# Hybrid block: the first two weight tiles multiply unscaled, transposed x; the normed h is made meanwhile

## The chip, the cores and the metric

One core of a Trainium2 chip runs the whole layer in one launch. The metric is the device time of one execution in microseconds (us), the median of several runs.

## The reference

One layer over 512 tokens of 1024 features in float32: RMS norm, a wide input projection, a state-space branch (SSD) and a windowed attention branch, their gated merge, then a mixture of 64 experts. What matters here is the head:

```python
h = rms_norm(x, norm1_g)          # x * rsqrt(mean(x*x) + 1e-6) per token, times norm1_g per feature
proj = h @ w_in
z, xbc, dt_raw, q, k, v, g_ssd, g_att = jnp.split(proj, IN_SPLITS, axis=-1)
# ssd_branch
xbc = conv(xbc, conv_w, 4 taps, per channel) + conv_b
xbc = silu(xbc)
dt = softplus(dt_raw + dt_bias)
```

The factor of a token, rsqrt(mean(x*x) + 1e-6), is the same for all its features, so it can be applied before or after the product with w_in.

## The kernel before, in words

The projections keep features on the partitions and the 512 tokens along the free axis. For float32 precision on TensorE, each operand is split in two float32r parts, hi (a rounded copy, made by ScalarE) and lo (the remainder, made by VectorE or GpSimd), and a product is hi\*hi + hi\*lo + lo\*hi: three matmuls for each of the eight blocks of 128 features, 24 for an output of 128 x 512.

A weight tile is 128 x 2048 (1 MB) and serves two such outputs, its two halves. `proj` (L185) loads one tile into a `w` buffer (two of them), splits each half (`split`, L178, into `g` buffers, four of them), runs the 24 matmuls (L196 to L198) into a PSUM buffer `mm` (two of them) and hands it to `use`. In `split` the remainder is GpSimd's for the first two splits and then for each fifth one, else VectorE's.

The head of the kernel (L144 to L174): x comes by rows, four row tiles of two 512-column halves. Squares are summed on ScalarE (L160) and VectorE (L157), the factor is made on VectorE and GpSimd (L161, L124, L125), the rows are scaled (L163, L164), 32 transposes on TensorE (L169) turn them, and L171 and L172 leave the eight pairs `hh`, `hl` of h, times norm1_g.

`dt_stage` (L210 to L273) follows: 16 matmuls of h with the weights of dt (L219, L220), four small transposes, and then a chain of small operations, mostly VectorE's, that ends in dt, its cumulative sums and their exponentials. Then `xbc_stage(0)` takes weight tiles 0, 1 and 2: each of their six outputs goes through `conv` (L280), which reads PSUM once on ScalarE and three times on VectorE (L283), then a tanh on ScalarE and a product on VectorE (L287). Only after the third VectorE read is the `mm` buffer free. `ssd_main(0)` needs all six and dt (first at L346). `gate_stage`, the next groups, attention, the merge and the output projection follow, and then the experts, whose weights (192 MB) SyncE loads at L779 into buffers that come free as the earlier stages end.

Tiles come from pools with a fixed number of buffers for each tag (`x`, `h` and `y` have 16, `c` six). A planner at build time orders each engine's instructions by the order in the program and by when it expects them to be ready, so that neighbouring stages are interleaved; on the chip each engine keeps that order. DMAs that are issued from SyncE go through one queue, in order.

Of the kernel before, what the change touches and what calls it, by code (L numbers as in the profile page):

```python
# [7 lines left out]
F = mybir.dt.float32  # L8
# [5 lines left out]
OP = mybir.AluOpType  # L14
# [16 lines left out]
def tile_hybrid(ctx: ExitStack, tc: tile.TileContext, x, pos, cols, rows, g2d, wrd, wdtd, wcm, wqkv, wso, wao, wo,  # L31
# [112 lines left out]
    xs_ = []  # L144
    st = pb.tile([128, 16], F, name="st")
    for t in range(4):
        xt = [x_(), x_()]
        for u in range(2):
            nc.sync.dma_start(xt[u], x[t * 128:(t + 1) * 128, u * 512:(u + 1) * 512])
        xs_.append(xt)  # L150
    wdt = v_(n=256)
    nc.sync.dma_start(wdt, wdtd)
    for t in range(4):
        for u in range(2):
            jk = c_()
            if u:
                V.scalar_tensor_tensor(jk, xs_[t][u], 1.0, xs_[t][u], op0=OP.mult, op1=OP.mult,  # L157
                                       accum_out=st[:, 2 * t + u:2 * t + u + 1])
            else:
                S.activation(jk, xs_[t][u], AF.Square, accum_out=st[:, 2 * t + u:2 * t + u + 1])  # L160
        V.tensor_tensor(st[:, 8 + t:9 + t], st[:, 2 * t:2 * t + 1], st[:, 2 * t + 1:2 * t + 2], op=OP.add)  # L161
        rsq(st[:, 8 + t:9 + t], 1, 1.0 / 1024)
        V.tensor_scalar(xs_[t][0], xs_[t][0], st[:, 8 + t:9 + t], None, op0=OP.mult)  # L163
        S.activation(xs_[t][1], xs_[t][1], AF.Copy, scale=st[:, 8 + t:9 + t])  # L164
    hh, hl = [], []
    for k in range(8):
        p = ptile(("tp", "sb", "y", "tp")[k // 2])
        for t in range(4):
            T.transpose(p[:, t * 128:(t + 1) * 128], xs_[t][k // 4][:, (k % 4) * 128:(k % 4 + 1) * 128], ident)  # L169
        hi, lo = h_(), h_()  # L170
        S.activation(hi, p, AF.Copy, scale=n1g[:, k:k + 1])  # L171
        V.scalar_tensor_tensor(lo, p, n1g[:, k:k + 1], hi.bitcast(F), op0=OP.mult, op1=OP.subtract)  # L172
        hh.append(hi)
        hl.append(lo)  # L174
# [9 lines left out]

    def proj(src, mh, ml, use):  # L185
        raw = w_()
        parts = 1 if nsp[0] else 2
        for i in range(parts):
            c = slice(i * 2048 // parts, (i + 1) * 2048 // parts)
            nc.sync.dma_start(raw[:, c], src[:, c])  # L190
        for hf in range(2):
            hi, lo = split(raw[:, hf * 1024:(hf + 1) * 1024], 1024)
            p = ptile("mm")
            for k in range(8):
                s = slice(k * 128, (k + 1) * 128)
                T.matmul(p, hi[:, s], mh[k], start=(k == 0), stop=False)  # L196
                T.matmul(p, hi[:, s], ml[k], start=False, stop=False)  # L197
                T.matmul(p, lo[:, s], mh[k], start=False, stop=(k == 7))  # L198
            use(hf, p)

# [9 lines left out]
    def dt_stage():  # L210
        wd = g_()
# [63 lines left out]
    dt_stage()  # L275

# [12 lines left out]
    def xbc_stage(g, qs=range(3)):  # L289
        for i in qs:  # L290
            def use(hf, p, i=i):
                c = 6 * g + 2 * i + hf
                tl = b_() if i == 0 else x_()
                if i == 0:
                    bc[g, hf] = tl
                else:
                    xsT[4 * g + 2 * (i - 1) + hf] = tl
                conv(c, tl, p)
            proj(wcm[3 * g + i], hh, hl, use)
# [340 lines left out]
    xbc_stage(0)  # L640
# [577 lines left out]
def _layout(inp):  # L1218
# [14 lines left out]
    def tm(m):  # L1233
# [20 lines left out]
        ("x", c(f["x"][0])),  # L1254
        ("pos", c(f["positions"][0].reshape(4, 128).T)),
# [31 lines left out]
```

## Time and profile before

| | |
|---|---|
| median of 3 runs | 1229.57 us (1229.18 to 1230.66) |
| the profiled execution | 1228.64 us, of which the span of the trace is 1226.8 us |
| TensorE busy | 1136.3 us (93%) |
| VectorE busy | 656.5 us (54%) |
| ScalarE busy | 388.6 us (32%) |
| GpSimd busy | 239.3 us (20%) |
| moved by DMA | 273.86 MB, 223 GB/s on average |

Times in the rows are in us from the start of the span. PE is TensorE's matmuls, PEld its weight loads, DVE VectorE, ACT ScalarE, POOL GpSimd, SPq SyncE's queue. A row of the timeline has start, duration, engine, line, operation, output and input; in brackets stands the engine's idle time just before and what ended it. Matmuls overlap, so their pitch is less than the duration shown. Engines' busy shares are averages over stages with different limits, so the stage at hand counts.

### The profile page before, as it was taken

The page shows a single profiled execution, that of the slowest core. Times are in us where ns is not written, and L with a number is a line of the kernel's source. Part 1 is how long each engine was busy: PE and PEld are TensorE (multiplying, and loading weights), DVE is VectorE, ACT ScalarE, POOL GpSimd, SP SyncE. Part 2 cuts the span into 40 slices and gives each one's busy share as a digit, 9 for nine tenths or more (in the row PEclk, how much of TensorE's full clock was granted, in tenths as well). Part 3 has the DMA queues.
Part 4 walks back from the last instruction along what each step waited for, and adds up shares of the span by engine and source line. Part 5 has one row for each costly group of instructions (what it writes and reads, how often), then busy time and mean ns, then how long its engine had stood idle before and what let it go on. Part 6 is the DMA issues. An engine that isn't in the chain of part 4 may idle for free.

```text
span 1226.8 us, 16583 instructions
## 1 busy us (share of the span) xinstructions
PE 1136.3 (93%) x6552; PEld 772.2 (63%) x6552; DVE 656.5 (54%) x1224; ACT 388.6 (32%) x796; POOL 239.3 (20%) x195
## 2 busy tenths in 40 slices
PE   6999999999999999999999959999897899999885
PEld 5777778877878988988778956443342434434321
DVE  5958584569536678877665464634422233331422
ACT  5456453464326455634432311110110011111000
POOL 3033431143024533330120241001001001000100
PEclk9999999999999999999999989999999899999999
DMA  4231213221221222222357257999999999999995
GB/s 157 98 118 38 100 61 129 94 79 54 83 104 35 70 104 87 87 69 69 137 168 300 110 235 305 419 420 420 420 419 421 420 415 398 387 420 419 421 419 221
DMA packets 43120, 273.86 MB, mean 223 GB/s; under 512 B 5024, under 2 KB 5664, under 8 KB 11808
## 3 DMA queue, kind: packets, MB, share of 16 engines
q1 hardware_dynamic: 39744, 263.34, 54.1%
q0 software_dynamic: 1712, 7.34, 1.6%
q10 hardware_dynamic: 1584, 2.10, 0.6%
q8 instruction: 52, 0.85, 0.3%
q14 instruction: 28, 0.23, 0.1%
HBM read 266.47 MB, written 6.29 MB: 222 GB/s over the span
## 4 chain that ended last, share of the span: by engine, by line
PE 77%; DVE 10%; DMA 8%; issue 2%; ACT 2%; POOL 1%; SPq 0%; DVEq 0%; ACTq 0%; POOLq 0%
PE mm L196 11%; PE mm L198 11%; PE mm L197 11%; PE mm L904 11%; PE y L925 5%; PE tp L884 5%; DMA rb<-in_wgu_dram 3%; PE tp L1003 3%; DVE acc L1005 2%; PE mm L481 2%; PE tp L1004 2%; PE mm L480 2%; DMA ra<-in_wdn_dram 2%; DMA rb<-in_wdn_dram 2%; PE mm L482 2%
## 5 line engine op out<-in xcount | busy, mean ns | idle before, releaser
L196 PE MATMUL mm<-h,g 128*128 128x512 f32 x448 | 180.7, 403 | 0.8 <-DVE c L309 0.5
L197 PE MATMUL mm<-h,g 128*128 128x512 f32 x448 | 179.8, 401 | 0.0
L198 PE MATMUL mm<-h,g 128*128 128x512 f32 x448 | 178.5, 399 | 0.8 <-POOL g L182 0.8
L904 PE MATMUL mm<-rb,st 128*32 128x512 f32 x712 | 145.6, 619 | 13.3 <-DMA rb<-in_wgu_dram 13.3
L181 ACT ACTIVATE g<-w 128x1024 fp32r<-128x1024 f32 x100 | 105.6, 1057 | 139.4 <-PE mm L197 99.0
L182 DVE TENSOR_TENSOR g<-w,g 128x1024 fp32r<-128x1024 f32 x78 | 98.7, 1265 | 72.9 <-ACT g L181 69.9
L1005 DVE TENSOR_TENSOR acc<-acc,tp 128x512 f32<-128x512 f32 x132 | 86.1, 684 | 37.2 <-PE tp L1004 37.0
L993 POOL TENSOR_SCALAR wk<-dr,vcol 128x512 fp32r<-128x512 int16 x17 | 26.6, 1565 | 383.8 <-PE tp L1004 347.9
L198 PEld LDWEIGHTS mm<-h,g 128*128 128x128 f32 x448 | 84.4, 188 | 22.2 <-POOL g L182 1.5
L196 PEld LDWEIGHTS mm<-h,g 128*128 128x128 f32 x448 | 84.5, 189 | 20.3 <-issue 1.2
L197 PEld LDWEIGHTS mm<-h,g 128*128 128x128 f32 x448 | 84.5, 189 | 19.8 <-issue 1.7
L182 POOL TENSOR_TENSOR g<-w,g 128x1024 fp32r<-128x1024 f32 x22 | 53.8, 2446 | 169.3 <-ACT g L181 138.5
L904 PEld LDWEIGHTS mm<-rb,st 128*32 128x32 f32 x712 | 30.9, 113 | 79.9 <-issue 55.8
L925 PE MATMUL y<-rb,n 128*32 128x512 f32 x384 | 72.0, 641 | 4.0 <-ACT n L916 3.3
L904 PE MATMUL mm<-ra,st 128*32 128x512 f32 x312 | 75.5, 597 | 0.0
L884 PEld LDWEIGHTS tp<-oh,hx 128*128 128x128 f32 x480 | 60.1, 191 | 23.6 <-issue 14.9
L931 DVE TENSOR_TENSOR yo<-y,yo 128x512 fp32r<-128x512 f32 x34 | 23.5, 691 | 92.3 <-ACT yo L930 92.3
L884 PE MATMUL tp<-oh,hx 128*128 128x256 f32 x480 | 66.7, 289 | 3.9 <-DVE m L956 3.6
L1003 PE MATMUL tp<-yo,wk 128*128 128x512 f32 x132 | 59.2, 465 | 11.1 <-DVE acc L1005 11.0
L1003 PEld LDWEIGHTS tp<-yo,wk 128*128 128x128 f32 x132 | 23.6, 187 | 69.6 <-DVE acc L1005 39.2
L909 ACT ACTIVATE n<-mm,gts 128x256 f32<-128x256 f32 x17 | 8.0, 473 | 180.6 <-PE mm L904 161.7
L910 DVE SCALAR_TENSOR_TENSOR n<-n,mm 128x256 f32<-128x256 f32 x17 | 7.1, 421 | 92.6 <-ACT n L909 92.6
(378 smaller groups left out, 2269.4 us busy)
## 6 DMA issues: line engine op xcount, KB each, us to landing
rb<-in_wgu_dram SPq DMA_DIRECT2D x89, 1024.0 KB, 15.1
rb<-in_wdn_dram SPq DMA_DIRECT2D x48, 1024.0 KB, 17.8
ra<-in_wgu_dram SPq DMA_DIRECT2D x39, 1024.0 KB, 12.5
w<-in_wcm_dram SPq DMA_DIRECT2D x27, 1024.0 KB, 4.9
ra<-in_wdn_dram SPq DMA_DIRECT2D x16, 1024.0 KB, 18.1
w<-in_wso_dram SPq DMA_DIRECT2D x8, 1024.0 KB, 4.9
w<-in_wqkv_dram SPq DMA_DIRECT2D x6, 1024.0 KB, 4.8
gtd<-c POOLq DMA_DIRECT2D x16, 256.0 KB, 2.5
```

The costliest lines, as they stand in the source:

```text
L181: S.activation(hi[:, :n], src, AF.Copy)
L182: (G if nsp[0] < 3 or nsp[0] % POOL_LO == 0 else V).tensor_tensor(lo[:, :n], src, hi[:, :n].bitcast(F), op=OP.subtract)
L196: T.matmul(p, hi[:, s], mh[k], start=(k == 0), stop=False)
L197: T.matmul(p, hi[:, s], ml[k], start=False, stop=False)
L198: T.matmul(p, lo[:, s], mh[k], start=False, stop=(k == 7))
L480: T.matmul(o, hh[k][:, ts], hi[:, s], start=(k == 0), stop=False)
L884: T.matmul(p[:, u * 256:(u + 1) * 256], hx[h][:, t, (k + u) * 128:(k + u + 1) * 128], oh[:, t], start=(h == 0 and t == 0), stop=(h == 1 an ...
L904: T.matmul(pg[e * 32:(e + 1) * 32], sts[u // 2][:, k, c:c + 32], wt[u, k // 4, e][:, (k % 4) * 512:(k % 4 + 1) * 512], start=(k == 0), sto ...
L925: T.matmul(py[n][e * 32:(e + 1) * 32], hT[:, f * 128 + e * 32:f * 128 + e * 32 + 32], wt[u, 2, e][:, ws], start=(f == 0), stop=(f == 1))
L993: G.tensor_scalar(wk, drow[0], vcol[:, b:b + 1], None, op0=OP.is_equal)
L1003: T.matmul(p, wk[:, t * 128:(t + 1) * 128], yhl[n][0], start=True, stop=False)
L1005: V.tensor_tensor(acc[t][:, ns], acc[t][:, ns], p, op=OP.add)
```

## The change

A copy of x, transposed outside (`xtd`: eight blocks of 128 features by 512 tokens), is a new input. The loads at the head are reordered: the first quarter of weight tile 0, two blocks of transposed x, the second quarter, the other six blocks, the second half of tile 0, then x by rows. The blocks times norm1_g, without the tokens' factors, are split into `fh`, `fl` (`y` buffers). Tile 0 is multiplied with these into two `y` buffers of PSUM, and so is tile 1, through `proj`. The sums of squares are taken from x by rows, all four factors in one go; a product of ones with the factors on a diagonal spreads them over the partitions (`rb_`). The outputs of tiles 0 and 1 are multiplied by `rb_` on their way out of PSUM (into a `c` buffer), and `conv` reads that. h is made from the transposed blocks, norm1_g and `rb_`, and split as before, with every second remainder on GpSimd. The 32 transposes are gone. `dt_stage` now stands behind tiles 0 and 1 and ahead of tile 2, and loads its own weights. From tile 2 on all is as before.

```diff
-    xs_ = []
     st = pb.tile([128, 16], F, name="st")
-    for t in range(4):
-        xt = [x_(), x_()]
-        for u in range(2):
-            nc.sync.dma_start(xt[u], x[t * 128:(t + 1) * 128, u * 512:(u + 1) * 512])
-        xs_.append(xt)
-    wdt = v_(n=256)
-    nc.sync.dma_start(wdt, wdtd)
+    xT, xs_, w0 = [x_() for k in range(8)], [[x_(), x_()] for t in range(4)], w_()
+    nc.sync.dma_start(w0[:, 0:512], wcm[0][:, 0:512])
+    nc.sync.dma_start(xT[0], xtd[0])
+    nc.sync.dma_start(xT[1], xtd[1])
+    nc.sync.dma_start(w0[:, 512:1024], wcm[0][:, 512:1024])
+    for k in range(2, 8):
+        nc.sync.dma_start(xT[k], xtd[k])
+    nc.sync.dma_start(w0[:, 1024:], wcm[0][:, 1024:])
     for t in range(4):
         for u in range(2):
...
+            nc.sync.dma_start(xs_[t][u], x[t * 128:(t + 1) * 128, u * 512:(u + 1) * 512])
+    wdt = v_(n=256)
...
+    fh, fl = [], []
+    for k in range(8):
+        if k in (0, 4):
+            if k == 0:
+                whi, wlo = g_(), g_()
+            c = slice(k * 128, (k + 4) * 128)
+            S.activation(whi[:, c], w0[:, c], AF.Copy)
+            G.tensor_tensor(wlo[:, c], w0[:, c], whi[:, c].bitcast(F), op=OP.subtract)
+        hi, lo = y_(), y_()
+        S.activation(hi, xT[k], AF.Copy, scale=n1g[:, k:k + 1])
+        V.scalar_tensor_tensor(lo, xT[k], n1g[:, k:k + 1], hi.bitcast(F), op0=OP.mult, op1=OP.subtract)
+        fh.append(hi)
+        fl.append(lo)
+    p0_ = [ptile("y"), ptile("y")]
+    triple(whi, wlo, fh, fl, p0_[0])
+    triple(*split(w0[:, 1024:], 1024), fh, fl, p0_[1])
+
+    for t in range(4):
+        for u in range(2):
+            jk, a = c_(), st[:, 2 * t + u:2 * t + u + 1]
+            if u:
+                V.scalar_tensor_tensor(jk, xs_[t][u], 1.0, xs_[t][u], op0=OP.mult, op1=OP.mult, accum_out=a)
+            else:
+                S.activation(jk, xs_[t][u], AF.Square, accum_out=a)
+    V.tensor_reduce(st[:, 8:12], st[:, 0:8].rearrange("p (t u) -> p t u", u=2), axis=AX.X, op=OP.add)
+    rsq(st[:, 8:12], 4, 1.0 / 1024)
+    dg, rb_ = v_(), v_()
+    for t in range(4):
+        V.tensor_scalar(dg[:, t * 128:(t + 1) * 128], ident, st[:, 8 + t:9 + t], None, op0=OP.mult)
+    p = ptile("sb")
+    T.matmul(p, ones, dg, start=True, stop=True)
+    S.activation(rb_, p, AF.Copy)
+    hh, hl = [], []
+    for k in range(8):
+        V.scalar_tensor_tensor(xT[k], xT[k], n1g[:, k:k + 1], rb_, op0=OP.mult, op1=OP.mult)
+        hi, lo = h_(), h_()
+        S.activation(hi, xT[k], AF.Copy)
+        (G if k % 2 else V).tensor_tensor(lo, xT[k], hi.bitcast(F), op=OP.subtract)
+        hh.append(hi)
+        hl.append(lo)
...
     def dt_stage():
+        nc.sync.dma_start(wdt, wdtd)
...
-    def xbc_stage(g, qs=range(3)):
+    def xbc_stage(g, qs=range(3), first=False):
         for i in qs:
             def use(hf, p, i=i):
                 c = 6 * g + 2 * i + hf
+                if first:
+                    u = c_()
+                    V.tensor_tensor(u, p, rb_, op=OP.mult)
+                    p = u
...
-            proj(wcm[3 * g + i], hh, hl, use)
+            if first and i == 0:
+                for hf in range(2):
+                    use(hf, p0_[hf])
+            elif first:
+                proj(wcm[3 * g + i], fh, fl, use)
+            else:
+                proj(wcm[3 * g + i], hh, hl, use)
...
-    xbc_stage(0)
+    xbc_stage(0, qs=(0, 1), first=True)
+    dt_stage()
+    xbc_stage(0, qs=(2,))
     ssd_main(0)
```

The 24 matmuls of an output moved into a helper, `triple`, with the same three lines as L196 to L198, and `proj` always loads its tile in one DMA (before, the first tile came in two).

## Rows read from the trace of the kernel before

**Rows 1.** Mean rates: busy us (x instructions) by engine, clock, DMA share, GB/s, in two stretches.
```profile
core 0: us, PE busy (x) PEld busy (x) DVE busy (x) ACT busy (x) POOL busy (x), PEclk, DMA share, GB/s
50.00:100.00 50.00, 50.00 (x239) 39.12 (x238) 33.44 (x64) 27.03 (x49) 11.43 (x10) 1.00 0.26 92
750.00:800.00 50.00, 48.51 (x307) 24.82 (x304) 25.25 (x56) 8.18 (x15) 6.35 (x5) 1.00 1.01 418
```

**Rows 2.** Waits of SyncE's queue, whole span: us in total, times, longest.
```profile
SPq L779 <- PE mm L738: 38.9, 2, 38.4
```

**Rows 3.** Waits of TensorE, first 60 us: us in total, times, longest.
```profile
PE tp L169 <- DVE x L163: 9.6, 3, 8.3
PE mm L198 <- POOL g L182: 0.8, 1, 0.8
```

**Rows 4.** Timeline of TensorE: start us, us, what, idle before and its releaser.
```profile
8.31 0.69 PE L169 MATMUL tp<-ident,x 128*128 128x128 f32 x2 [8.31 <-DVE x L163]
...
15.57 0.66 PE L219 MATMUL mm<-h,g 128*128 128x512 f32 x1
...
28.42 0.50 PE L198 MATMUL mm<-h,g 128*128 128x512 f32 x1 [0.76 <-POOL g L182]
28.76 0.40 PE L196 MATMUL mm<-h,g 128*128 128x512 f32 x1
...
45.41 0.47 PE L196 MATMUL mm<-h,g 128*128 128x512 f32 x1 [0.32 <-DVE v L246]
```

**Rows 5.** Loads, first 20 us: GB/s in 40 slices; then ScalarE's wait for the third piece.
```profile
GB/s 0 0 0 74 91 216 242 364 267 174 210 211 269 395 410 397 406 414 397 408 404 352 393 385 442 467 385 459 426 344 98 16 0 0 0 0 0 0 0 0
...
7.06 0.63 ACT L160 ACTIVATE c<-x 128x512 f32<-128x512 f32 x1 [1.94 <-DMA x<-in_x_dram]
```

**Rows 6.** Timeline of VectorE: from a row tile's last square to its scaling.
```profile
5.91 0.69 DVE L157 SCALAR_TENSOR_TENSOR c<-x 128x512 f32<-128x512 f32 x1 [1.11 <-DMA x<-in_x_dram]
...
7.77 0.49 DVE L163 TENSOR_SCALAR x<-x,st 128x512 f32<-128x512 f32 x1 [0.71 <-POOL st L125]
```

**Rows 7.** What one operation costs: four from the timeline, then the line of L414.
```profile
13.90 2.58 POOL L182 TENSOR_TENSOR g<-w,g 128x1024 fp32r<-128x1024 f32 x1 [0.17 <-ACT g L181]
15.41 1.05 ACT L181 ACTIVATE g<-w 128x1024 fp32r<-128x1024 f32 x1
17.74 1.40 DVE L172 SCALAR_TENSOR_TENSOR h<-sb,colt,h 128x512 fp32r<-128x512 f32 x2
...
34.80 1.23 DVE L182 TENSOR_TENSOR g<-w,g 128x1024 fp32r<-128x1024 f32 x1
...
L414 PE MATMUL sb<-v,one x8: 592/592/696, 173.9 to 490.9; 128*128 128x512 f32 x8
```

**Rows 8.** A VectorE product beside GpSimd's split, then line L421: min/median/max ns.
```profile
39.91 0.28 DVE L245 TENSOR_TENSOR v<-v 128x128 f32<-128x128 f32 x1
...
40.41 2.40 POOL L182 TENSOR_TENSOR g<-w,g 128x1024 fp32r<-128x1024 f32 x1 [12.04 <-ACT g L181]
40.49 2.46 DVE L245 TENSOR_TENSOR v<-v 128x128 f32<-128x128 f32 x1
...
L421 DVE TENSOR_TENSOR y<-v,y x16: 679/684/2892, 177.8 to 499.5; 128x512 fp32r<-128x512 f32 x16
```

**Rows 9.** Busy time by engine in two stretches; columns as in group 1.
```profile
20.00:30.00 10.00, 9.02 (x41) 6.67 (x40) 4.70 (x8) 2.71 (x4) 2.37 (x1) 1.00 0.08 12
30.00:40.00 10.00, 10.00 (x44) 8.03 (x43) 9.76 (x25) 4.15 (x7) 0.00 (x0) 1.00 0.52 194
```

**Rows 10.** Timeline: last read of convolution tile 5 in PSUM, and TensorE's next use.
```profile
62.89 0.75 DVE L283 SCALAR_TENSOR_TENSOR x<-mm,colt,x 128x509 f32<-128x509 f32 x1
...
65.23 0.39 PE L196 MATMUL mm<-h,g 128*128 128x512 f32 x1
```

**Rows 11.** Timeline of VectorE: end of the dt chain, and its first use.
```profile
45.76 0.29 DVE L249 SCALAR_TENSOR_TENSOR dt<-v 128x128 f32<-128x128 f32 x1
...
70.21 0.69 DVE L346 TENSOR_TENSOR x<-tp,dt 128x512 f32<-128x512 f32 x1 [1.91 <-PE tp L345]
```

More of the change, by code (lines that the diff above doesn't have):

```diff
@@ L30, in tile_hybrid @@
 @with_exitstack
-def tile_hybrid(ctx: ExitStack, tc: tile.TileContext, x, pos, cols, rows, g2d, wrd, wdtd, wcm, wqkv, wso, wao, wo,
+def tile_hybrid(ctx: ExitStack, tc: tile.TileContext, x, xtd, pos, cols, rows, g2d, wrd, wdtd, wcm, wqkv, wso, wao, wo,
                 wgu, wdn, out):
@@ L141, in c_ @@
     def c_(dt=F, n=512): return pc.tile([128, n], dt, name="c", tag="c", bufs=6, padded_shape=[128, 512])
-    xs_ = []
     st = pb.tile([128, 16], F, name="st")
-    for t in range(4):
-        xt = [x_(), x_()]
-        for u in range(2):
-            nc.sync.dma_start(xt[u], x[t * 128:(t + 1) * 128, u * 512:(u + 1) * 512])
-        xs_.append(xt)
-    wdt = v_(n=256)
-    nc.sync.dma_start(wdt, wdtd)
+    xT, xs_, w0 = [x_() for k in range(8)], [[x_(), x_()] for t in range(4)], w_()
[6 more added lines that the diff above has]
+    nc.sync.dma_start(w0[:, 1024:], wcm[0][:, 1024:])
     for t in range(4):
         for u in range(2):
[L155 to L174, printed above, removed]
+            nc.sync.dma_start(xs_[t][u], x[t * 128:(t + 1) * 128, u * 512:(u + 1) * 512])
+    wdt = v_(n=256)
     nsp = [0]
@@ L183, in split, with triple @@
         return hi, lo
+    def triple(hi, lo, mh, ml, p):
+        for k in range(8):
+            s = slice(k * 128, (k + 1) * 128)
+            T.matmul(p, hi[:, s], mh[k], start=(k == 0), stop=False)
+            T.matmul(p, hi[:, s], ml[k], start=False, stop=False)
+            T.matmul(p, lo[:, s], mh[k], start=False, stop=(k == 7))
     def proj(src, mh, ml, use):
         raw = w_()
[L187 to L190, printed above, removed]
+        nc.sync.dma_start(raw, src)
         for hf in range(2):
@@ L193, in proj @@
             p = ptile("mm")
[L194 to L198, printed above, removed]
-            use(hf, p)
+            triple(hi, lo, mh, ml, p)
+            use(hf, p)
+    fh, fl = [], []
[30 more added lines that the diff above has]
+    hh, hl = [], []
+    for k in range(8):
+        V.scalar_tensor_tensor(xT[k], xT[k], n1g[:, k:k + 1], rb_, op0=OP.mult, op1=OP.mult)
[4 more added lines that the diff above has]
+        hl.append(lo)
     dt = pb.tile([128, 128], F, name="dt")
@@ L273, in dt_stage @@
         V.tensor_tensor(aT[32:64], pt[32:64], hv[32:64].bitcast(F), op=OP.subtract)
-    dt_stage()
     bc, xsT = {}, {}
@@ L1254, in _layout @@
         ("x", c(f["x"][0])),
+        ("xt", c(f["x"][0].T.reshape(8, 128, 512))),
         ("pos", c(f["positions"][0].reshape(4, 128).T)),
```

## The prediction

> **What bounds the kernel now.** I read the mean rates of long stretches first, to see which engine is full where. From 50 us on TensorE is busy 50.00 us of 50, while the DMA engines are at a quarter; from 750 us on the DMA share is 1.01 at 418 GB/s, and it stays so almost to the end [rows 1]. So there are two halves: projections bound by TensorE, then expert weights bound by transfers. The second view is what SyncE's queue waits for: the first large block of expert loads waits 38 us for TensorE (a product of w_out, line 738) [rows 2]. The loads can't start before TensorE is through with the first half, so a microsecond that TensorE gains or loses early should arrive at the end one to one.
>
> The third view is TensorE's own waits in the first 60 us, and the fourth its timeline. It first starts at 8.31 us, on transposes; the first product with weights starts at 15.57; the last wait in the ramp is for GpSimd's split, and ends at 28.42 [rows 3, 4]. After that only 0.32 us is lost up to 45.41. From 28.76 to 45.09 there are 21 products of tile 0 and 48 of tile 1, so one takes 16.33 / 69 = 0.237 us.
>
> The measure I use is TensorE's lost time: the clock when it comes out of its last early wait, less its useful products at 0.237 us. By 28.42 it had done 24 + 2 products of tile 0, 16 of dt, and dt's four small transposes, which I count as two products: 44 x 0.237 = 10.4. Lost: 28.42 - 10.4 = 18.0 us. The transposes of x are in this, and so cost nothing of their own: 24 of 32 lie ahead of 15.57, the others between products that wait for h.
>
> **The change part by part.**
>
> *The new loads.* The third 256-KB piece is there at 7.06, and from about 6.5 us on the queue moves some 400 GB/s [rows 5], 0.655 us for each piece. Piece n is then there at 7.06 + (n - 3) x 0.655. In the new order the last of xT is piece 10 (11.65), the second half of tile 0 is complete with piece 12 (12.95), the last of x is piece 20 (18.2), tile 1 is complete with piece 24 (20.8). The load of wdt moves behind tile 1 on the same queue, 128 KB for work that now comes 20 us later: no cost. If it were queued behind a load that waits for a buffer, dt would wait too.
>
> *First tile.* Its first half is paced by xT and finishes by about 14 us. The second half needs ScalarE's copy (1.05) and GpSimd's remainder (2.40 to 2.58, I take 2.45) [rows 7, 8]: 12.95 + 1.05 + 2.45 = 16.45. By then 26 products are done, 6.2 us: lost 10.3. The other 22 take 5.2, to 21.65.
>
> *Row factors.* From the last square to the scaled tile took 7.77 - 5.91 = 1.86 us [rows 6]. Here: 18.2 + 1.86, four diagonal scalings of some 0.2, the product with ones (two records of 0.59 that overlap [rows 7]; from 0.6 to 1.2, I take 0.9), and a copy of 0.63: the broadcast factors are there at 22.4. The product with ones sits in TensorE's queue, with the second tile behind it: 0.9 lost, TensorE at 22.55. GpSimd's power waits for the sums, and tile 1's split is queued behind it, but that isn't due yet. ScalarE's copy of the factors waits for the product, and tile 1's second copy is queued behind it, due only at 29.
>
> *Second tile.* 20.8 + 1.05 + 2.45 = 24.3 for its first remainder, and TensorE arrives there at 22.55 + 0.5: 1.3 lost. Sum so far: 10.3 + 0.9 + 1.3 = 12.5. The first half then lasts to 24.3 + 22 x 0.237 = 29.5, and two more products to 30.0.
>
> *The new work on VectorE.* The remainder of tile 1's second half is VectorE's (1.23 [rows 7]), and h stands ahead of it there: eight products and four subtractions at 0.66 (half of two for 1.40, less their overlap [rows 7]), 7.9 us. They can't start before 22.4, nor perhaps before GpSimd's split ends at 24.3: a VectorE product of two SBUF operands that took 0.28 us took 2.46 beside such a split and ended with it, and one of line 421 took 2892 ns instead of 684 [rows 8]. So the remainder is ready at 22.4 + 7.9 + 1.2 = 31.5, or at 33.4: TensorE waits 1.5 to 3.4. The end below is no wait at all, if the planner puts the remainder ahead of h. The end above adds GpSimd's four subtractions for h, half of 2.40 each, 4.8 in all, if each of them holds VectorE: 8.2. I take 2.5, the middle of the inner two, since VectorE also has products that read PSUM to put beside GpSimd. Lost: 12.5 + 2.5 = 15.0.
>
> The Trainium skill states this rule, in "SBUF — State Buffer", section "SBUF: two separate sides": VectorE and GpSimd hold a port pair in turn, for a whole instruction, and the other blocks fully. The trace agrees (2.46 us for 0.28). It speaks against the change, which makes the first VectorE work SBUF to SBUF and gives GpSimd six more operations; by it alone the upper end would hold.
>
> *dt.* Its 16 products move behind tile 1, when h is there; its long VectorE chain, which now ends at 45.76 and is first needed at 70.21 [rows 11], starts some 18 us later and keeps about 6 of its 24 us of slack. That hides it; without that cover TensorE would wait at line 345.
>
> *Splits.* One split fewer goes through the helper, so GpSimd's fifth ones shift by a tile. Either engine is covered by the products of a tile ahead; I charge nothing, with 1.2 us (2.40 less 1.23) either way where one isn't.
>
> **The sum.** Lost 18.0 before and 15.0 after: 3.0 us gained, with 5.5 (no wait on VectorE) and -2.7 (wait 8.2) as ends. The profiled execution, a span of 1226.8 in 1228.64, becomes 1225.6. It lies 0.93 under the median, so the median becomes 1229.57 - 3.0 = 1226.6.
>
> **Rivals.**
>
> *The whole head start is kept.* The remainder goes ahead of h, or h hides it: gain 5.5, time 1224.1. For it: before 28 us VectorE was far from full, 4.70 of 10 from 20 to 30 [rows 9]. Against it: that is just where h is put.
>
> *The port eats it.* About half of GpSimd's subtractions block VectorE, the wait at tile 1 is 5.5, lost is 18.0, and nothing is gained: 1229.6. For it: rows 8. It is also what is left where the change does what it says and TensorE merely waits later instead of earlier.
>
> *VectorE becomes the bound, and the kernel is slower.* From 30 to 40 us VectorE is busy 9.76 of 10 [rows 9], and TensorE already lost 0.32 to it [rows 4]. The convolution's last read of tile 5 in PSUM ends at 62.89 + 0.75 = 63.64, and the product that takes that buffer starts at 65.23 [rows 10]: 1.6 us of margin. After the factors come, VectorE has 7.9 us of h and four products of 0.66 to scale what leaves PSUM, 10.5 in all, and before had 5.3 idle in that stretch: 5.2 too much, less one split of 1.2, so 4.0. That is 2.4 over the margin, and the dt chain now runs among the same convolutions. If little of h fits into the gap, TensorE stands at the gate's products some 3 us later than now: 1232.5. It decides from the point where VectorE has no idle time from the factors to tile 5.
>
> **How the numbers follow.** The forecast has 0.48, the whole head start 0.12, the port 0.20, VectorE as the bound 0.20. 0.2% is 2.5 us, about what a measurement of this kernel tells from no change. Faster: 0.12, and 0.36 of the forecast (it lies close to the limit). Same: 0.12 of the forecast and most of the port's. Slower: VectorE as the bound and a little of the port's. The range runs from 1223.0, 1.1 under the whole head start (one split's 1.2), to 1232.5.
>
> **What would show it.** TensorE's first product near 7 us, its wait on GpSimd ending near 16.5, another near 24, and then one on VectorE of 1.5 to 3.4 us before tile 1's second half. The products of tile 2 should start about 3 us ahead of 45.41 + dt's place in the order, and the DMA stretch near 750 shift by the same 3. It is wrong if TensorE waits between 30 and 75 us for convolutions or dt, if VectorE's h products last several times 0.66 us beside GpSimd, or if the planner's new order opens gaps after 75 us, where before there were next to none.

## The result and the profile after

The changed kernel takes 1257.2 us (median of 4 runs, 1255.03 to 1261.33), the kernel before 1229.38 on the same chip: ratio 1.0232, 95% interval 1.0216 to 1.0249. It is slower by 27.8 us. The forecast was 1226.6, and its range ended at 1232.5. The profiled execution of after took 1256.84 us; its span of 1255.1 is 28.3 longer than the 1226.8 of before.

First, where along the span the loss arises. SyncE's loads of `w_so` wait for buffers that the first half frees, so the first of them is a clock for TensorE's progress. Its row in the timeline (start, duration, queue, what) in before and after, and under each the busy time of every engine up to that moment (columns as in [rows 1]):

```profile
269.96 0.33 SPq L190 DMA_DIRECT2D w<-in_wso_dram  x1
0.00:269.96 269.96, 258.97 (x1252) 203.50 (x1253) 176.15 (x293) 133.15 (x243) 78.98 (x75) 1.00 0.27 95
```
```profile
291.79 0.33 SPq L176 DMA_DIRECT2D w<-in_wso_dram  x1
0.00:291.79 291.79, 262.80 (x1233) 203.91 (x1233) 192.16 (x304) 138.65 (x254) 91.14 (x78) 0.96 0.27 95
```

Of the 28.3 us, 21.8 are lost by there (at the first `w_ao` load it is 25.5, at the first large block of expert loads 25.2). TensorE stood idle for 291.79 - 262.80 = 29.0 us instead of 269.96 - 258.97 = 11.0, which is 18.0 more, and was busy 3.8 longer, although the 32 transposes of before, some 7.4 us of its busy time, are gone. The next two views say when. TensorE's waits up to that load in after (us in total, times, longest), to set against [rows 3]:

```profile
PE mm L245 <- DVE c L319: 13.0, 1, 13.0
...
PE tp L386 <- POOL v L384: 3.4, 2, 2.0
```

and rates by stretches of 10 us in after (columns as in [rows 1]; the two rows of [rows 9] are the same stretches in before):

```profile
20.00:30.00 10.00, 9.22 (x38) 6.68 (x38) 8.65 (x23) 4.40 (x7) 3.94 (x3) 1.00 0.59 220
30.00:40.00 10.00, 6.39 (x29) 4.96 (x27) 9.84 (x14) 5.73 (x10) 9.04 (x4) 1.00 0.15 62
40.00:50.00 10.00, 0.56 (x1) 0.50 (x2) 8.04 (x17) 4.63 (x7) 0.00 (x0) 0.50 0.00 0
50.00:60.00 10.00, 10.00 (x37) 7.99 (x36) 8.51 (x9) 3.67 (x7) 2.82 (x1) 0.82 0.05 9
...
100.00:110.00 10.00, 7.70 (x29) 4.85 (x28) 2.33 (x4) 2.51 (x4) 2.46 (x2) 0.91 0.30 100
110.00:120.00 10.00, 8.26 (x51) 5.59 (x49) 8.55 (x15) 5.78 (x16) 3.79 (x3) 0.92 0.02 7
120.00:130.00 10.00, 8.07 (x38) 5.91 (x37) 7.00 (x11) 6.47 (x18) 3.98 (x3) 0.83 0.00 0
```

The extra idle time adds up from two places. One wait of 13.05 us ends at 49.44; from 100 to 130 us TensorE idles another 30 - 24.03 = 5.97, where before it was never idle. Less the 0.7 by which the first 30 us improved (10.67 us idle before, 9.98 after), and the 0.32 of [rows 4] that is gone, that is the 18.0. The third column from the right, the granted clock, falls in the stretches in and behind these two holes, so a part of the longer work lies there.

TensorE's timeline in after (start, duration, what, idle before and its releaser), against [rows 4]:

```profile
7.50 0.80 PE L170 MATMUL y<-y,g 128*128 128x512 f32 x1 [7.50 <-ACT y L193]
...
18.10 0.50 PE L172 MATMUL y<-y,g 128*128 128x512 f32 x1 [1.70 <-POOL g L164]
...
26.11 0.50 PE L172 MATMUL mm<-y,g 128*128 128x512 f32 x1 [0.78 <-POOL g L164]
...
36.01 0.39 PE L172 MATMUL mm<-y,g 128*128 128x512 f32 x1
49.44 0.76 PE L245 MATMUL mm<-h,g 128*128 128x512 f32 x1 [13.05 <-DVE c L319]
```

So the head start is real. By 26.11 there are 48 + 4 products done, 52 x 0.237 = 12.3 us, and 13.8 are lost by the prediction's measure, where before 18.0 were. Tiles 0 and 1 are through at 36.4, without a wait on VectorE. Then the next product in the order is dt's, and it stands for 13 us. VectorE's timeline in that time, and GpSimd's four remainders of h:

```profile
26.14 1.21 DVE L164 TENSOR_TENSOR g<-w,g 128x1024 fp32r<-128x1024 f32 x1
...
27.36 5.38 DVE L219 SCALAR_TENSOR_TENSOR x<-x,colt,v 128x512 f32<-128x512 f32 x8
...
33.86 4.06 DVE L222 TENSOR_TENSOR h<-x,h 128x512 fp32r<-128x512 f32 x3
...
38.91 0.68 DVE L222 TENSOR_TENSOR h<-x,h 128x512 fp32r<-128x512 f32 x1
...
39.61 0.74 DVE L307 SCALAR_TENSOR_TENSOR b<-c,colt,b 128x511 f32<-128x511 f32 x1
40.27 0.41 DVE L242 TENSOR_TENSOR g<-v,g 128x256 fp32r<-128x256 f32 x1
...
46.37 2.32 DVE L307 SCALAR_TENSOR_TENSOR b<-c,colt,b 128x511 f32<-128x511 f32 x3 [0.30 <-ACT b L305]
48.61 0.68 DVE L319 TENSOR_TENSOR c<-mm,v 128x512 f32<-128x512 f32 x1
...
29.51 9.53 POOL L222 TENSOR_TENSOR h<-x,h 128x512 fp32r<-128x512 f32 x4 [3.45 <-ACT h L221]
```

dt's product needs three things. h is there at 39.6. The remainder of dt's weights (L242) stands behind h and ends at 40.7. Last comes a free `mm` buffer of PSUM: it holds tile 1's first half, and the scaling that empties it (L319, at 48.61) stands behind tile 0's two convolutions.

The second hole begins with dt itself. Its last operation, and its first use in the state-space step, after (before: [rows 11]):

```profile
77.62 0.29 DVE L275 SCALAR_TENSOR_TENSOR dt<-v 128x128 f32<-128x128 f32 x1
...
97.40 0.68 DVE L380 TENSOR_TENSOR x<-tp,dt 128x512 f32<-128x512 f32 x1
```

dt ends 31.9 us later than before and is first used 27.2 later. The matmuls of group 1's first tiles, which stood beside that step before, are spent by 103.5, so the step's waits, such as `PE tp L386 <- POOL v L384` above, stand bare.

### The profile page after: what moved, and what is told of

The parts are those of the page before. It is cut to its first block, busy times and chain, and to the rows that moved or that the text cites. A ratio compares the mean times of both kernels' runs of the same rounds, so it can differ in the third digit from the quotient of the medians.

```text
span 1255.1 us, 16551 instructions
## 1 busy us (share of the span) xinstructions
PE 1147.9 (91%) x6522; PEld 775.3 (62%) x6522; DVE 668.4 (53%) x1234; ACT 392.6 (31%) x802; POOL 248.8 (20%) x197
## 4 chain that ended last, share of the span: by engine, by line
PE 77%; DMA 10%; DVE 8%; ACT 1%; issue 1%; POOL 1%; SPq 0%; DVEq 0%; POOLq 0%
PE mm L170 11%; PE mm L172 11%; PE mm L171 11%; PE mm L940 9%; PE y L961 6%; PE tp L920 4%; DMA rb<-in_wgu_dram 4%; DMA ra<-in_wdn_dram 3%; PE tp L1039 3%; DMA rb<-in_wdn_dram 2%; PE mm L515 2%; PE mm L514 2%; DVE acc L1041 2%; PE mm L516 2%; PE tp L1040 2%; PE y L424 1%
## 5 line engine op out<-in xcount | busy, mean ns | idle before, releaser
L170 PE MATMUL mm<-h,g 128*128 128x512 f32 x416 | 168.7, 406 | 3.3 <-DVE x L307 1.9
L172 PE MATMUL mm<-h,g 128*128 128x512 f32 x416 | 167.3, 402 | 0.0
L171 PE MATMUL mm<-h,g 128*128 128x512 f32 x416 | 167.3, 402 | 0.0
L1041 DVE TENSOR_TENSOR acc<-acc,tp 128x512 f32<-128x512 f32 x132 | 86.1, 684 | 39.7 <-PE tp L1040 39.6
L1029 POOL TENSOR_SCALAR wk<-dr,vcol 128x512 fp32r<-128x512 int16 x17 | 26.6, 1565 | 384.2 <-PE tp L1040 348.6
L170 PEld LDWEIGHTS mm<-h,g 128*128 128x128 f32 x416 | 79.2, 190 | 23.2 <-DVE x L307 2.2
L172 PEld LDWEIGHTS mm<-h,g 128*128 128x128 f32 x416 | 79.1, 190 | 19.6 <-issue 1.0
L171 PEld LDWEIGHTS mm<-h,g 128*128 128x128 f32 x416 | 79.2, 190 | 18.0 <-issue 0.8
L961 PE MATMUL y<-rb,n 128*32 128x512 f32 x384 | 76.3, 659 | 3.8 <-ACT n L952 3.3
L940 PE MATMUL mm<-ra,st 128*32 128x512 f32 x312 | 72.9, 597 | 0.0
L1039 PE MATMUL tp<-yo,wk 128*128 128x512 f32 x132 | 59.4, 466 | 11.5 <-DVE acc L1041 11.4
L170 PE MATMUL mm<-y,g 128*128 128x512 f32 x144 | 57.3, 398 | 0.0
## 6 DMA issues: line engine op xcount, KB each, us to landing
rb<-in_wgu_dram SPq DMA_DIRECT2D x89, 1024.0 KB, 16.6
```

The lines of the kernel that those rows point to most:

```text
L940: T.matmul(pg[e * 32:(e + 1) * 32], sts[u // 2][:, k, c:c + 32], wt[u, k // 4, e][:, (k % 4) * 512:(k % 4 + 1) * 512], start=(k == 0), sto ...
L961: T.matmul(py[n][e * 32:(e + 1) * 32], hT[:, f * 128 + e * 32:f * 128 + e * 32 + 32], wt[u, 2, e][:, ws], start=(f == 0), stop=(f == 1))
L1029: G.tensor_scalar(wk, drow[0], vcol[:, b:b + 1], None, op0=OP.is_equal)
L1039: T.matmul(p, wk[:, t * 128:(t + 1) * 128], yhl[n][0], start=True, stop=False)
L1041: V.tensor_tensor(acc[t][:, ns], acc[t][:, ns], p, op=OP.add)
```

## The experiments

All were run against the kernel before, which stood at 1229.68 to 1229.93 beside them. The result in one table; the last three columns are the starts of dt's last operation, of its first use and of the first `w_so` load, from each trace.

| kernel | median us | ratio (95%) | dt | use | w_so |
|---|---|---|---|---|---|
| before | 1229.38 | | 45.8 | 70.2 | 270.0 |
| after | 1257.2 | 1.0232 (1.0216 to 1.0249) | 77.6 | 97.4 | 291.8 |
| e4_dt_later | 1247.26 | 1.0135 (1.0118 to 1.0152) | 72.3 | 92.2 | 284.1 |
| e7_dt_later_xbuf | 1240.14 | 1.0090 (1.0073 to 1.0107) | 70.7 | 90.6 | 281.3 |
| e8_after_xbuf | 1258.3 | 1.0228 (1.0211 to 1.0245) | 76.5 | 96.3 | 292.0 |
| e2_scale_first | 1247.76 | 1.0155 (1.0130 to 1.0180) | 72.0 | 91.7 | 283.8 |
| e1_hl_vector | 1251.82 | 1.0194 (1.0172 to 1.0217) | 76.5 | 96.3 | 289.4 |
| e3_one_tile | 1249.5 | 1.0160 (1.0143 to 1.0177) | 71.2 | 90.1 | 286.1 |
| e5_dt_unscaled | 1255.9 | 1.0222 (1.0205 to 1.0239) | 71.8 | 91.4 | 288.0 |
| e6_dt_tile1_h | 1251.19 | 1.0165 (1.0147 to 1.0183) | 70.2 | 90.2 | 288.2 |
| e9_dt_weights_early | 1247.76 | 1.0146 (1.0125 to 1.0166) | 69.5 | 87.4 | 283.2 |
| e10_three_fixes | 1247.75 | 1.0147 (1.0130 to 1.0164) | 72.8 | 92.9 | 284.9 |
| e11_before_load | 1242.52 | 1.0102 (1.0081 to 1.0123) | 58.2 | 79.2 | 282.0 |
| e12_after_short_dt | 1380.64 | (other work in the second half) | 71.2 | 87.8 | 286.0 |
| e13_before_short_dt | 1356.23 | (other work in the second half) | 34.5 | 70.1 | 269.4 |

My theory after the first look: dt has lost its place, and what it costs is the state-space step standing bare. The rivals: tile 1's scaling, held up in VectorE's order, with the wait of 13 us; and the port, that is GpSimd's subtractions holding up VectorE.

**dt's place alone (`e4_dt_later`).** In the kernel before, only the call of `dt_stage` moves to where the change has it.

```diff
-    dt_stage()
-    xbc_stage(0)
+    xbc_stage(0, qs=(0, 1))
+    dt_stage()
+    xbc_stage(0, qs=(2,))
```


> The kernel before with nothing but dt's stage moved behind tiles 0 and 1. Late-dt theory (part of the loss is the move itself): TensorE shows waits for the state-space step of group 0 that the kernel before doesn't have, 5 to 8 us, time 1235 to 1238. Order theory alone: dt's move costs nothing, its chain had 24 us of slack, 1228 to 1231.

It loses 17.6 us, more than the 5 to 8 that were expected. dt's row, TensorE's waits of the first 150 us, and the busy times up to the first `w_so` load (columns as in [rows 1]):

```profile
72.32 0.29 DVE L249 SCALAR_TENSOR_TENSOR dt<-v 128x128 f32<-128x128 f32 x1
...
PE tp L350 <- POOL v L348: 3.5, 2, 2.0
PE mm L196 <- ACT h L171: 2.0, 1, 2.0
...
PE mm L196 <- DVE b L281: 1.5, 1, 1.5
PE mm L196 <- DVE x L281: 1.5, 1, 1.5
...
0.00:284.12 284.12, 264.99 (x1252) 207.78 (x1253) 173.81 (x293) 133.33 (x243) 79.73 (x75) 0.99 0.26 91
```

There is the same wait in the state-space step as in after (3.5 us against 3.4), there are convolutions that free `mm` late, and there is no 13-us wait. But the ramp isn't as before: dt's 16 products no longer stand between those that wait for h, and TensorE waits 2.0 us for h. At 28.66 us 29 products are done, so 21.8 us are lost by the prediction's measure, 3.8 more than before; the changed kernel, whose ramp is filled with tile 0, doesn't lose these. Of the 14.2 us at the first `w_so` load this leaves some 9 for the step that stands bare (1.2 go to the convolution near 35 us). Only 5.2 of them are idle time, from 100 to 150 us. The rest of them, like a part of what the ramp loses, is work that takes longer: the same 1252 matmuls are busy for 264.99 us instead of 258.97. So late dt by itself makes some 9 of the changed kernel's 21.8 us at that load, an estimate from these numbers.

**The hand-out of x buffers in that step (`e7_dt_later_xbuf` and `e8_after_xbuf`).** The four scaled inputs of group 0 go into `a` buffers, so that the convolutions of the next group need not wait for them: once on top of the kernel with dt moved, once in the changed kernel.

```diff
-        xdt = [x_() for c in range(4)]
+        xdt = [x_() if g else a_() for c in range(4)]
```


> The kernel before with dt moved behind tiles 0 and 1 (as e4_dt_later, 1247.3), and the four scaled inputs of the state-space step of group 0 in idle buffers of another pool instead of x buffers. Buffer theory (dt's move is dear because the convolutions of group 1 get their x buffers only after those four steps, which wait for dt, and hold the PSUM that TensorE's next tile needs): most of the 17 us come back, 1231 to 1237. Chain theory (TensorE's order itself has the state-space step bare, buffers or not): 1244 to 1248.

> The changed kernel with the same other buffers as e7_dt_later_xbuf. Buffer theory: the later loss near 104 to 122 us goes, 8 to 14 us come back, 1243 to 1249. Chain theory: 1254 to 1258.

It gives back 7.1 of 17.6 us in the first, between the two ranges expected, and nothing that can be told in the second. In the first, 2.8 of them are there at the first `w_so` load, and the last of the step's four uses of dt comes at 106.9 instead of 109.5; the rest is gained further on. In the changed kernel the first use moves by 1.1 us, from 97.4 to 96.3, and the `w_so` load not at all. So the buffers are a part of what late dt costs where all else is early, and no part of it in the changed kernel; why not is not settled.

**The scalings first (`e2_scale_first`).** In the changed kernel the four scalings that empty PSUM are put ahead of the four convolutions.

```diff
                 if first:
                     u = c_()
                     V.tensor_tensor(u, p, rb_, op=OP.mult)
-                    p = u
+                    late.append((c, i, hf, u))
+                    return
...
     xbc_stage(0, qs=(0, 1), first=True)
+    late_convs()
     dt_stage()
```


> The changed kernel with the four scalings out of PSUM written ahead of the four convolutions. Order theory: the scaling of tile 1's first half is done right after its products and after h (about 40 us instead of 49.3), so TensorE's wait ahead of dt falls from 13 to 2 to 5 us, its clock doesn't fall, and 10 to 12 us come back if nothing later takes them: 1245 to 1247. Port theory: h is still what is late, wait 8 to 13 us, 1252 to 1257. Late-dt theory (the state-space step stands bare because dt ends at 78 instead of 46): the later loss near 104 to 122 us stays, as dt isn't moved; the convolutions now stand between, so at most 10 us are gained.

9.4 us come back, 8.0 of them by the first `w_so` load. TensorE's wait ahead of dt's product is now for the remainder of dt's weights:

```profile
PE mm L245 <- DVE g L242: 6.5, 1, 6.5
```

So half of the 13 us was the PSUM buffer, and behind it stands the next thing on VectorE, which comes after h.

**The port (`e1_hl_vector`).** All of h's remainders go to VectorE.

```diff
-        (G if k % 2 else V).tensor_tensor(lo, xT[k], hi.bitcast(F), op=OP.subtract)
+        V.tensor_tensor(lo, xT[k], hi.bitcast(F), op=OP.subtract)
```


> The changed kernel with all eight remainders of h on VectorE, none on GpSimd. Port theory (GpSimd's four subtractions, 9.5 us instead of some 5, hold VectorE back and so cause the 13 us wait of TensorE ahead of dt): h takes about 16 x 0.61 = 9.8 us on VectorE instead of 12.2, the wait shrinks by some 2.5 us or more, time 1253 to 1255. If the port were the main cause, the wait would fall under 5 us and the time under 1249. Order theory (the wait comes from the scaling of tile 1 standing on VectorE behind two convolutions): the wait stays above 10 us, time 1254 to 1257.

5.4 us come back, 2.4 of them by the first `w_so` load; where the others arise was not looked into. The 1251.82 lie a little under both ranges expected, while the wait stayed above 10 us as the order theory said. VectorE's remainders, now eight, in this kernel's timeline:

```profile
32.66 3.08 DVE L222 TENSOR_TENSOR h<-x,h 128x512 fp32r<-128x512 f32 x5
...
36.74 1.22 DVE L222 TENSOR_TENSOR h<-x,h 128x512 fp32r<-128x512 f32 x2
37.99 0.68 DVE L222 TENSOR_TENSOR h<-x,h 128x512 fp32r<-128x512 f32 x1
```

Eight take 4.98 us; in after four took 4.74 beside GpSimd. Sharing them with GpSimd saved VectorE 0.24 us. The wait ahead of dt is still 12.7: the port costs something, but it is not the main term.

**Only one tile ahead of the factors (`e3_one_tile`).** Tile 0 alone is multiplied unscaled, then dt, then tiles 1 and 2 from h.

```diff
-    xbc_stage(0, qs=(0, 1), first=True)
+    xbc_stage(0, qs=(0,), first=True)
     dt_stage()
-    xbc_stage(0, qs=(2,))
+    xbc_stage(0, qs=(1, 2))
```


> The changed kernel with only weight tile 0 multiplied unscaled; dt and tiles 1 and 2 take h. No product's buffer then waits for a convolution before dt. Order theory: TensorE waits only for h itself, from about 22.5 to 28 us, and then runs; dt starts at 28 to 30 instead of 49; time 1230 to 1236. Port theory: h's second half still comes at 38 us, dt is paced by it, 8 us lost there: 1236 to 1242. Late-dt theory: dt is nearly where it was before, so the loss near 104 to 122 us is gone.

Two scalings are gone and dt comes one tile earlier in the order, and 7.7 us come back; the 1249.5 lie above all three ranges expected. dt's last operation still stands at 71.2, since TensorE now waits 11.4 us for L242 behind h: it has run out of work that doesn't need h. The chain from the factors to dt is on VectorE, whichever tiles TensorE has.

**dt from the unscaled operands (`e5_dt_unscaled`).** dt needn't wait for h if it too is scaled on its way out of PSUM. Its weights then sit in two `a` buffers, and the stage stands ahead of tiles 0 and 1 again.

```diff
-            T.matmul(p, w3[:, k, :], hh[k], start=(k == 0), stop=False)
-            T.matmul(p, w3[:, k, :], hl[k], start=False, stop=(k == 7))
+            T.matmul(p, w3[k // 4][:, k % 4, :], fh[k], start=(k == 0), stop=False)
+            T.matmul(p, w3[k // 4][:, k % 4, :], fl[k], start=False, stop=(k == 7))
...
-        S.activation(dtT[0:64], p[0:64], AF.Copy)
+        V.tensor_tensor(dtT[0:64], p[0:64], rb_[0:64], op=OP.mult)
...
+    dt_stage()
     xbc_stage(0, qs=(0, 1), first=True)
-    dt_stage()
```


> The changed kernel with dt taken from the unscaled operands too and scaled on its way out of PSUM, so that its stage can stand ahead of tiles 0 and 1 again, as before the change (its weights in two spare buffers). Late-dt theory (14 to 17 us of the loss come from dt's move alone): the waits of TensorE for the state-space step of group 0, near 104 to 122 us, are gone, and 14 to 17 of the 28 us come back: 1239 to 1244. What is left is the wait for tile 1's scaling behind the convolutions, now ahead of tile 2 instead of dt, 8 to 13 us. Order theory alone: little changes, 1252 to 1257, as that wait only moves.

The next kernel orders the program as dt, tile 1 with the scalings, h (all on VectorE), convolutions:

```diff
     dt_stage()
     xbc_stage(0, qs=(0, 1), first=True)
+    make_h()
+    late_convs()
```


> As e5_dt_unscaled, and the work written in the order in which TensorE needs it: dt, tile 1 and the four scalings, then h (all on VectorE), then the four convolutions, then tile 2. If the loss is dt's place, the scalings' place and the port together, all three are gone: TensorE waits only in the ramp (lost time some 13 us instead of 18) and for h at most 2 us: 1224 to 1229. If VectorE has simply too much to do up to the convolution of tile 2 whatever its order, TensorE waits there 4 to 10 us: 1231 to 1240.

And the third also loads and splits dt's weights at the very start:

```diff
+    wdt = v_(n=256)
+    nc.sync.dma_start(wdt, wdtd)
     nc.sync.dma_start(w0[:, 1024:], wcm[0][:, 1024:])
...
+    for z in range(2):
+        G.memset(wd[z].bitcast(F), 0.0)
...
+        V.tensor_tensor(w3[z][:, :, 32:64], r3[:, 4 * z:4 * z + 4], w3[z][:, :, 0:32].bitcast(F), op=OP.subtract)
```


> As e6_dt_tile1_h, with dt's weights loaded ahead of tile 0's second half and split ahead of the squares, so that its 16 products can stand right behind tile 0 (in e6 they waited 9.8 us for those weights' remainder on VectorE, behind h). Dt theory (the state-space step of group 0 starts about 20 us after dt is ready, and when it starts too late TensorE runs out of products to put between): dt is ready at 45 to 52 us, the waits near 100 to 122 us are gone, and TensorE waits only in the ramp: 1226 to 1234. If VectorE is full from the factors to tile 2 whatever the order, dt or the convolutions come late again: 1238 to 1248.

They take 1255.9, 1251.19 and 1247.76 us (`e5_dt_unscaled`, `e6_dt_tile1_h`, `e9_dt_weights_early`). The first is where it was expected if dt's place costs nothing, but dt came only 5.8 us earlier in it, so it says little of that. The second lies above both of its ranges, the third at the upper end of the range for a full VectorE. In the first two TensorE still waits 9.7 and 9.8 us for dt's weights behind other work of VectorE. In the third dt's products are done by 20.1, before the factors exist, and dt still ends only at 69.8. Rates of that kernel from 26 to 70 us, and the first and last of VectorE's operations for dt:

```profile
26.00:70.00 44.00, 33.86 (x134) 26.41 (x134) 42.83 (x93) 24.68 (x36) 4.99 (x3) 0.88 0.21 72
...
34.49 0.67 DVE L250 TENSOR_TENSOR v<-mm,v 64x512 f32<-64x512 f32 x1
...
69.50 0.29 DVE L277 SCALAR_TENSOR_TENSOR dt<-v 128x128 f32<-128x128 f32 x1
```

VectorE is busy 42.83 of 44 us: what it does earlier makes something else later. But dt's own operations are only some 8 of these 44 us; they stand among convolutions and remainders because the planner puts them there. No run has them first on VectorE, so whether an order that serves dt first would help was not tested.

**Three repairs at once.** The scalings first, h's remainders on VectorE, and dt ahead of the convolutions (`e10_three_fixes`; the second part of the diff is against `e2_scale_first`):

```diff
-        (G if k % 2 else V).tensor_tensor(lo, xT[k], hi.bitcast(F), op=OP.subtract)
+        V.tensor_tensor(lo, xT[k], hi.bitcast(F), op=OP.subtract)
...
     xbc_stage(0, qs=(0, 1), first=True)
-    late_convs()
     dt_stage()
+    late_convs()
```


> The changed kernel with the scalings ahead, h's remainders all on VectorE, and dt (still from h) written ahead of the four convolutions instead of behind. The scalings alone gave 9.4 us (1247.8) and the port 5.4; if these add and dt comes some 5 us earlier: 1238 to 1243. If the port's share was only in the wait that the scalings' place already removed: 1245 to 1249, since dt still ends near 65 us or later and the state-space step stays bare.

1247.75, the same as the scalings first by themselves. The single gains of 9.4 and 5.4 don't add.

**The load alone (`e11_before_load`).** Into the kernel before, with its order untouched, come sixteen idle products of VectorE just ahead of dt:

```diff
+    for k in range(16):
+        V.tensor_tensor(c_(), hh[k % 8].bitcast(F), hh[k % 8].bitcast(F), op=OP.mult)
     dt_stage()
```


> The kernel before, with sixteen idle VectorE products of 128x512 (results thrown away) put ahead of dt_stage, where the change has h and the scalings: at 0.6 to 0.66 us each some 10 us of VectorE, no change of order, nothing new on GpSimd or the port. Theory 1 (what costs is VectorE full while dt and the first convolutions wait for it): dt ends 8 to 10 us later, near 55, its chain of small TensorE steps is that much later, and the kernel is 4 to 10 us slower, 1234 to 1240. Theory 2 (dt can be late within what is left of its way to line 346; what costs is dt's place behind two weight tiles, as in e4): 1230 to 1232, since VectorE was busy only 4.70 of 10 us from 20 to 30.

12.6 us are lost, more than the first theory expected. dt's last operation stands at 58.17, 12.4 later. One sentence of the expectation was wrong, that nothing would be new at the port: GpSimd's split and VectorE's products beside it in this kernel's timeline, then TensorE's waits, the first of which was 0.8 us before:

```profile
25.07 4.90 DVE L276 TENSOR_TENSOR c<-h 128x512 f32<-128x512 f32 x8
...
30.08 2.63 DVE L276 TENSOR_TENSOR c<-h 128x512 f32<-128x512 f32 x1
...
25.92 6.24 POOL L182 TENSOR_TENSOR g<-w,g 128x1024 fp32r<-128x1024 f32 x1 [9.68 <-PE mm L220]
...
PE mm L198 <- POOL g L182: 4.6, 1, 4.6
PE mm L196 <- DVE x L285: 2.6, 1, 2.6
```

So TensorE's wait for the split is 3.8 us longer by the port, and behind it nine starts of products are 0.43 us apart instead of 0.24 (32.81 to 36.65), another 1.7. That is 5.5 of the 12.1 us at the first `w_so` load; the rest goes with late convolutions and late dt together. VectorE is full from 20 to 30 us here (10.00 of 10), but busy only 6.36 of the next 10. So the run shows that more load on VectorE suffices for a loss of this size, nearly half of it by way of the port; it doesn't isolate dt.

**A shorter dt (`e12_after_short_dt` and `e13_before_short_dt`).** The last pair comes closest to isolating it: the same 14 small operations of dt's polynomial are left out of the changed kernel and of the kernel before. This also takes their 3.6 us off VectorE.

```diff
-        for c in (13, 11, 9, 7, 5, 3, 1):
-            V.tensor_tensor(q, q, s2, op=OP.mult)
-            V.tensor_scalar(q, q, 1.0 / c, None, op0=OP.add)
```


> The changed kernel with the seven steps of dt's polynomial left out (14 small VectorE operations, 3.6 us of busy time, which with convolutions between them take 69.2 to 77.3 us in its trace); dt's values are then not the reference's. Theory 1 (dt's end sets when the state-space step of group 0 starts, and that step then stands bare): dt ends near 70 instead of 77.6, the first scaled input near 90 instead of 97.4, and 4 to 7 of the 28 us come back, 1250 to 1253. Theory 2 (by the time dt is there, what holds that step is the convolutions of tiles 1 and 2 and the x buffers): the first scaled input moves by less than half of that, and the time stays at 1255 to 1257.

> The control for the run with the short dt: the kernel before with the same seven steps left out (dt's values are not the reference's). If the 24 us from dt's end to its first use are slack, nothing changes: 1229 to 1230. If they are a chain that begins when dt ends, dt ends some 6 us earlier, near 40, and the first scaled input moves with it; whether that is worth time in a kernel whose TensorE hardly waits there is open: 1225 to 1230, and I expect 1228.

Other values of dt send other tokens to the experts, and both kernels then move some 10.8 MB more in the second half; their times (1380.64 and 1356.23) don't compare with the others, so the first `w_so` load is read instead. dt and its first use in the changed kernel with the short dt, and that load; below them the same rows of its control:

```profile
71.23 0.28 DVE L272 SCALAR_TENSOR_TENSOR dt<-v 128x128 f32<-128x128 f32 x1
...
87.79 0.69 DVE L377 TENSOR_TENSOR x<-tp,dt 128x512 f32<-128x512 f32 x1 [4.74 <-PE tp L376]
...
285.99 0.33 SPq L176 DMA_DIRECT2D w<-in_wso_dram  x1
```
```profile
34.46 0.29 DVE L246 SCALAR_TENSOR_TENSOR dt<-v 128x128 f32<-128x128 f32 x1
...
70.10 0.69 DVE L343 TENSOR_TENSOR x<-tp,dt 128x512 f32<-128x512 f32 x1 [2.74 <-PE tp L342]
...
269.38 0.33 SPq L190 DMA_DIRECT2D w<-in_wso_dram  x1
```

In the changed kernel dt ends 6.4 us earlier, its first use comes 9.6 earlier, and the load 5.8 earlier. In the control dt ends 11.3 us earlier, the first use 0.1 and the load 0.6. In the changed kernel the wait of 3.4 us in the state-space step (for L384 in after) is gone, too. So in the changed kernel an earlier dt, with the lighter VectorE that comes with it, moves TensorE nearly one to one, and in the kernel before not at all. That the first use moves by more than dt shows that the lighter VectorE has a share; the pair doesn't separate the two. The 13-us wait, which stays at 13.1 in the run with the short dt, is no part of these 5.8.

## Why the prediction was wrong

*What bounds the kernel: right.* The two halves stand, and SyncE's first expert loads still wait 36.8 us for TensorE (38.4 in [rows 2]). "One to one" was nearly right: 21.8 us late at the first `w_so` load became 28.3 at the end.

*Loads and first tile: right to 1.8 us.* First product at 7.50 (predicted near 7), the wait on GpSimd's split ends at 18.10 (16.45), the next at 26.11 (24.3). Lost time there is 13.8 (12.5). The last of x came at about 20 instead of 18.2.

*Row factors: late by 2.6.* They were put at 22.4; ScalarE's copy ends at 25.0. x's later arrival carries 1.8 of it.

*The remainder of tile 1's second half: wrong place.* The prediction put it behind h and took a wait of 2.5. The planner put it ahead of h ([rows 9] showed VectorE at 4.70 of 10 there; after, 8.65), so there was no such wait. The work of h, 5.38 + 4.74 = 10.1 us instead of 7.9, had to be paid at the next product that needs VectorE, and that was dt's. Asking for one instruction's place in a queue, and not for the sum of what the queue must do before TensorE runs out of other work, was the first error.

*"dt … keeps about 6 of its 24 us of slack. That hides it": the step that failed.* It put dt's move at nothing, and has three errors. dt's 16 products were to run behind tile 1; they waited 13.05 us, in the end for the `mm` buffer of tile 1's first half, whose release behind VectorE's queue had no term in the sum. The delay of dt's end was put at 18 us and came to 31.9, since dt also waited for h, for its weights behind h, for a PSUM buffer, and for convolutions that stand between its small operations. And the 24 us of [rows 11] were no slack. From dt's end to its first use passes a chain of cumulative sums, transposes and products; each is on TensorE's queue behind a group of 24 products (in after they start at 83.43, 89.50 and 96.22). In the kernel with dt moved it takes 19.9 us, in after 19.8, in the shortened one 16.6: so some 5 to 8 of the 24 were slack. The control shows the other side: dt 11 us earlier moved its first use by 0.1. Moving dt alone, 26.6 us later, costs 17.6, of which some 4 are the ramp's. The fallback clause, that "TensorE would wait at line 345", named the right stage: the waits stand in the state-space step.

*Port: mechanism right, half of the upper end's price, place different.* The upper end held 4.8 us for GpSimd's four subtractions. VectorE's four remainders beside them took 4.74 us instead of 4 x 0.66, so VectorE lost 2.1, and sharing saved it 0.24 us of 4.98. The Trainium skill, "SBUF — State Buffer", section "SBUF: two separate sides", says that the one of the two engines that starts first has the port pair for its whole instruction. The trace agrees as far as one blocks the other: in the load run the split, 2.40 us in [rows 8], took 6.24, and a VectorE product that took 0.61 alone took 2.63. There the split first stood behind several VectorE products in a row, from 25.92 to 29.97. That 5.4 us come back at the end of the kernel without GpSimd's share of h, near the 4.8, is no proof of that size: only 2.4 of them are there at the first `w_so` load, and the port had no wait of TensorE of its own, but was one of several things in VectorE's queue.

*Rival "VectorE becomes the bound": nearest to what came, price a tenth.* Its condition, no idle time of VectorE from the factors to tile 5, is nearly met by the row with 42.83 of 44 us, for the kernel in which dt's products wait for nothing; in after, with its hole on TensorE, VectorE is busy 38.95 of the same 44. It was priced only at the hand-out of `mm` buffers, 2.4 us over a margin, and said of dt merely that its chain "now runs among the same convolutions". One of its terms was misread, too: from 22.4 to 63.64 us VectorE had 7.3 us idle in before (busy 33.93 of 41.24) and not 5.3, which is the one gap that ends at 27.05; with 7.3 only 0.4 us are over the margin. What it missed is that dt's product and dt's chain stand in the same queue as the new work.

*No term for slower work.* The sum held product time fixed at 0.237. Of the clock two pieces can be counted: eight starts of products 0.43 us apart behind the 13-us wait, 1.5 us, and six from 122.61 on, 1.1 us.

How the 28 us divide: up to the first `w_so` load the ramp gains 4.2 us by the prediction's measure (18.0 to 13.8), and 0.3 of idle time is saved. Against it stand 13.05 of wait ahead of dt's product, 5.97 of idle time in the bare step, and so 7.3 of work that takes longer, 2.6 of it the clock as counted above; the sum is 21.8. Another 3.7 come up to the first `w_ao` load and 2.8 behind it, and no run takes these apart. What can be taken away singly is 9.4 (scalings' order) and 5.4 (port), and the short dt gives 0.9 us for each us. These overlap, and their exact shares stay open. So does a form of the change that gains: none here beat the kernel before, and none had dt's operations first on VectorE.

## What to carry to other kernels

Before moving work to fill an engine's ramp, add up what every other engine must do between the same two points, and find the first product of the filled engine that needs that sum. A long gap between a result and its first use is slack only as far as no chain runs in it: follow the chain, or make the result earlier and see whether anything moves. A scaling that is moved to the way out of PSUM makes the buffer's release wait for the factors and for the queue in front of it.

## What was not expected of the hardware

TensorE's granted clock fell in this wait, to 0.50 in the stretch from 40 to 50 us, which is 1.2 of 2.4 GHz, after it had stood idle since 36.4. It worked slowly when it came back; starts of the first products behind the wait, in after:

```profile
50.43 0.63 PE L245 MATMUL mm<-h,g 128*128 128x512 f32 x1
50.86 0.63 PE L246 MATMUL mm<-h,g 128*128 128x512 f32 x1
...
54.19 0.40 PE L245 MATMUL mm<-h,g 128*128 128x512 f32 x1
54.43 0.39 PE L246 MATMUL mm<-h,g 128*128 128x512 f32 x1
```

They start 0.43 us apart, later 0.24. From 50.00 to 53.42 there are eight such steps, 8 x 0.19 = 1.5 us. The first products of the kernel, from 8.88 on, also came 0.43 us apart, up to 12.30, where the row gives a granted clock of 1.00, so that the reason isn't shown: this head start, with eight such steps, is worth 1.5 us less than its products count.

GpSimd pays at the port too, not VectorE alone: its four remainders of 128x512 took 9.53 us, 2.4 each, while VectorE made its own. A remainder of that size at the start of after took half of this:

```profile
6.41 1.26 POOL L191 TENSOR_TENSOR g<-w,g 128x512 fp32r<-128x512 f32 x1 [3.38 <-ACT g L190]
```
